# A tuned hybrid-encoder kernel: the final norm of four token tiles done in place between the pieces of a product, residual stores put behind loads, pooled tokens loaded one product sooner

## The chip, the cores and the metric

The kernel runs on one core of a Trainium2 chip. The metric is the time of the core in device microseconds (us) for one execution. TensorE (PE), VectorE (DVE), ScalarE (ACT) and GpSimd (POOL) work side by side, each through its own instructions in order; SyncE (SP) issues nearly all transfers (DMAs), in order too.

## The reference, cut to what matters

One layer with 1024 tokens of 1024 channels, all in float32:

```python
h = rmsnorm(x, norm_mix)
q, k, v, r, lr_f, lr_b, u, g_a, g_b = split(h @ w_in)
y_a = (gla(forward) + gla(backward), normed per head, gated) @ w_branch_gla   # branch A
y_b = (multiscale_pool(u) @ w_pool_group[g], per group g) * pool_scale        # branch B
x = x + (sigmoid(g_a) * y_a + sigmoid(g_b) * y_b) @ w_out
h2 = rmsnorm(x, norm_ffn)
x = x + (silu(h2 @ w_gate) * (h2 @ w_up)) @ w_ffn_out                          # w_ffn_in = [w_gate | w_up]
out = rmsnorm(x, norm_final)       # x * rsqrt(mean(x^2) + eps) * norm_final, per token
```

## The kernel before

Every large product is done by a seven-product scheme on 2 x 2 blocks of both operands, numbered 1 to 7; sums and differences of blocks are formed beside the matmuls. Each of the seven works on operands split in two parts, high and low (`wh`/`wl`, `gh`/`gl`, `oh`/`ol`, `ph`/`pl`): ScalarE casts the high part, VectorE or GpSimd subtracts it from the source to give the low part (`split_to`, L197 and L198), and TensorE takes three matmuls (high x high, low x high, high x low) for one product of tiles (L271, `mm3`). Each matmul is 128x512.

The stages, in the profile's time: norm, projections and attention to about 360 us; the gate units, among which the pooled branch is mixed in (`Gates`, to about 580); the branch product and the merged product with the residual, to about 743; the FFN's gate and up products (`Gated`, to about 1200); and the seven products of the FFN's output, each in six pieces (five of 24 matmuls and one of 12), in the order 1, 2, 6, 5, 3, 7, 4, to about 1384. Then comes the last of the final norm.

The order of instructions on each engine is written by hand: the program's order is the order of each engine. After each `mm3` a counter `pump` goes on by one and releases put-off steps (`soon(delay, step)` puts a step off by so many products) and the next steps of generators that run beside the products (`begin(generator, delay)`; each `yield` gives the number of products until its next step). Tiles come from pools that are given round: 39 slots of 4 KB for each partition (`slot`), five scratch tiles (`t2`), six weight tiles. Whoever writes a tile waits for all who used it before, a store that has not landed among them. On SyncE each DMA also waits until the one eight places before it has landed.

Three places of this program are touched:

- **The gate units** (L1346 on). The run of unit n has seven products; `load_pooled(n - 6)` (L1242) loads the two parts `ph`, `pl` of a group of pooled tokens from `p_out` (L1245), for which `Gates.run` then mixes small products `yb` (ScalarE copies a product's bank to `ga`, L1304; VectorE adds, L1309). Beside the gate units, steps prepare FFN weights: GpSimd forms sums, ScalarE casts `uph` (L630) into a scratch tile, VectorE subtracts `upl` (L621), SyncE stores both to `u_out` (L617). These are a ring through the five `t2` tiles.
- **The residual and the second norm.** `collect_out` adds the merged product to `x2`, squares it on ScalarE (`squares`, L1578) and calls `normed`, which scales `x2` into `xn` (VectorE, for the last tile ScalarE, L1598) and lists a store of `x2` to `x_out`; `flush` issues these stores (L501). `features` (L1520 on) then transposes `xn` on TensorE in groups of four (L1530), ScalarE moves each bank to `hb` (L1533), VectorE forms differences (L1545, L1548), ScalarE casts `gh` (L1511), VectorE or GpSimd subtracts `gl` (L1515). `features(1)` begins 12.7 products late. Unit products copy and add into `g` (L1667, L1669) and apply Silu (L1670).
- **The final norm.** After product 3 tiles 0 to 3 are complete. `whole(t)` (L1810) squares both halves of `x2`, and after a delay forms the scale (`two_scale`: VectorE adds, GpSimd takes the power -0.5) and multiplies by scale and gain into an output slot `res` (L1822, two halves), which is stored whole (L1825). Beside this run product 7's pieces, whose operands are loaded as `wor` and `gor` (L1741, L1742), cast (`oh`) and split, the weight's `ol` by VectorE, the activation's by GpSimd. Tiles 4 to 7 are done in halves after products 7 and 4 (`second_half`, `first_half`).

## Time and profile before

| | |
|---|---|
| median of 3 runs | 1393.41 us (1392.92 to 1393.5) |
| the profiled execution | 1393.17 us, span 1391.4 us |
| granted TensorE clock, mean | 0.998 |
| DMA moved | 243.60 MB, mean 175 GB/s |

A timeline row has the start and duration in us, the engine, the line, the operation, what is written from what, and how many like it were joined (x); in brackets the idle time of the engine ahead of it and what ended that. A windows row has the stretch, its length, each engine's busy time and count (PE, PEld, DVE, ACT, POOL), the granted clock of TensorE, the busy share of the DMA engines and GB/s.

### The profile page before, as it was taken

The numbers are of one execution on the slowest core, as the hardware profiler recorded it, in microseconds if no ns is written. First come the engines' busy times: TensorE is split into PE (matmuls) and PEld (weight loads), VectorE is DVE, ScalarE is ACT, GpSimd is POOL, SyncE is SP. The second block draws the span as 40 slices with busy tenths as digits, with TensorE's granted clock in tenths as the row PEclk, the third lists the DMA queues.
The fourth block names the chain that finished last, engine by engine and source line by source line (L and its number), as shares of the span: only waits on it lengthen the run. The fifth ranks groups of instructions, "written<-read, shape, count | busy, mean of one in ns | idle before, by whom it ended". The sixth has DMA issues, their size and how long they took to land. (4 is left out here: it accounts for less than half of the span.)

```text
span 1391.4 us, 18166 instructions
## 1 busy us (share of the span) xinstructions
PE 1367.6 (98%) x6485; PEld 1143.5 (82%) x6485; DVE 837.3 (60%) x1018; ACT 645.5 (46%) x1176; POOL 750.1 (54%) x556
## 2 busy tenths in 40 slices
PE   8999999999999999999999999999999999999998
PEld 6788999988888888788887788888888888888876
DVE  6364656557736876678783865556556555344464
ACT  6465766655334445554347533333333334443243
POOL 3222717232298546568655276666666667564354
PEclk9999999999999999999999999999999999999999
DMA  6111413312488667996416355555544447965461
GB/s 224 31 53 54 147 60 128 107 47 75 136 242 281 200 209 255 373 403 222 165 57 242 114 174 174 174 175 174 162 151 138 146 142 271 395 246 187 166 238 64
DMA packets 166587, 243.60 MB, mean 175 GB/s; under 512 B 10937, under 2 KB 95969, under 8 KB 166497
## 3 DMA queue, kind: packets, MB, share of 16 engines
q1 hardware_dynamic: 166352, 242.18, 51.3%
q8 instruction: 51, 0.84, 0.2%
q14 instruction: 40, 0.32, 0.1%
q10 hardware_dynamic: 144, 0.26, 0.0%
HBM read 164.55 MB, written 77.86 MB: 174 GB/s over the span
## 5 line engine op out<-in xcount | busy, mean ns | idle before, releaser
L198 POOL TENSOR_TENSOR wl<-fs,wh 128x512 fp32r<-128x512 f32 x120 | 165.8, 1385 | 154.7 <-ACT wh L197 101.8
L271 PE MATMUL ps<-gh,wh 128*128 128x512 f32 x616 | 240.5, 390 | 1.2 <-DVE g L1669 0.6
L271 PE MATMUL ps<-gl,wh 128*128 128x512 f32 x616 | 239.8, 389 | 0.8 <-DVE gl L1515 0.8
L271 PE MATMUL ps<-gh,wl 128*128 128x512 f32 x616 | 239.8, 389 | 0.0
L198 POOL TENSOR_TENSOR wl<-fraw,wh 128x512 fp32r<-128x512 f32 x90 | 129.0, 1433 | 67.5 <-ACT wh L197 59.4
L271 PE MATMUL ps<-hh,wh 128*128 128x512 f32 x376 | 151.7, 403 | 0.0
L271 PE MATMUL ps<-hh,wl 128*128 128x512 f32 x376 | 146.8, 390 | 0.6 <-POOL wl L198 0.6
L271 PE MATMUL ps<-hl,wh 128*128 128x512 f32 x376 | 146.6, 390 | 0.0
L198 POOL TENSOR_TENSOR ol<-gor,oh 128x1024 fp32r<-128x1024 f32 (+1 forms) x42 | 104.5, 2496 | 77.3 <-ACT oh L197 70.3
L271 PEld LDWEIGHTS ps<-gh,wh 128*128 128x128 f32 x616 | 115.7, 188 | 25.9 <-DVE g L1669 0.9
L271 PEld LDWEIGHTS ps<-gl,wh 128*128 128x128 f32 x616 | 115.6, 188 | 24.6 <-DVE gl L1515 1.1
L271 PEld LDWEIGHTS ps<-gh,wl 128*128 128x128 f32 x616 | 115.6, 188 | 24.3 <-DMA wl<-u_out 0.3
L271 PE MATMUL ps<-ol,oh 128*128 128x512 f32 x308 | 120.7, 392 | 2.0 <-DVE ol L198 2.0
L271 PE MATMUL ps<-oh,ol 128*128 128x512 f32 x308 | 120.5, 391 | 0.0
L271 PE MATMUL ps<-oh,oh 128*128 128x512 f32 x308 | 120.4, 391 | 0.0
L198 POOL TENSOR_TENSOR wl<-raw,wh 128x512 fp32r<-128x512 f32 x40 | 54.6, 1377 | 116.2 <-ACT wh L197 107.8
L198 POOL TENSOR_TENSOR wl<-wraw,wh 128x512 fp32r<-128x512 f32 x56 | 89.9, 1632 | 45.6 <-ACT wh L197 45.5
L198 DVE TENSOR_TENSOR ol<-wor,oh 128x1024 fp32r<-128x1024 f32 (+1 forms) x42 | 68.2, 1653 | 47.1 <-ACT oh L197 44.4
L197 ACT CAST wh<-fs 128x512 fp32r<-128x512 f32 x120 | 73.8, 615 | 29.8 <-DVE fs L935 26.3
L271 PEld LDWEIGHTS ps<-hh,wl 128*128 128x128 f32 x376 | 70.6, 188 | 16.2 <-POOL wl L198 1.1
L271 PEld LDWEIGHTS ps<-hh,wh 128*128 128x128 f32 x376 | 70.7, 188 | 13.3 <-ACT wh L197 0.4
L271 PEld LDWEIGHTS ps<-hl,wh 128*128 128x128 f32 x376 | 70.8, 188 | 13.0
(260 smaller groups left out, 3114.5 us busy)
## 6 DMA issues: line engine op xcount, KB each, us to landing
fraw<-in_w_ffn_in_dram SPq DMA_DIRECT2D x44, 512.0 KB, 5.9
gor<-g_out SPq DMA_DIRECT2D x35, 512.0 KB, 5.4
g_out<-s SPq DMA_DIRECT2D x44, 256.0 KB, 2.3
raw<-in_w_in_dram SPq DMA_DIRECT2D x40, 256.0 KB, 4.9
fraw<-in_w_in_dram SPq DMA_DIRECT2D x20, 512.0 KB, 6.6
wor<-t_out SPq DMA_DIRECT2D x20, 512.0 KB
g_out<-g SPq DMA_DIRECT2D x33, 256.0 KB, 2.4
x<-in_x_dram SPq DMA_DIRECT2D x16, 512.0 KB, 4.6
```

The costliest lines, as they stand in the source:

```text
L197: nc.scalar.copy(hi, src)
L198: eng.tensor_tensor(lo, src, as_f32(hi), op=ALU.subtract)
L271: nc.tensor.matmul(ps, a[i], b[j], start=first and n == 0, stop=last and n == 2, skip_group_check=onto)
```

## The change

It makes four edits.

1. `load_pooled` for groups 0 and up is called ahead of the third product of a run, not behind it. On SyncE this moves rows in one place, in the run of unit 8. SyncE there before (`u_out` are stores of prepared weights, `ph` and `pl` the loads of pooled tokens, `yb_out` stores):

```order
L617 DMA u_out_6_517<-uph_5327 128x512
L617 DMA u_out_6_517<-upl_5328 128x512
L617 DMA u_out_3_514<-uph_5358 128x512
L617 DMA u_out_3_514<-upl_5359 128x512
L1245 DMA ph_5401<-p_out 128x1024
L1245 DMA pl_5402<-p_out 128x1024
L501 DMA yb_out<-ga_5128 256x1x512
L501 DMA yb_out<-ga_5151 256x1x512
```

SyncE at the same place now:

```order
L1245 DMA ph_5375<-p_out 128x1024
L1245 DMA pl_5376<-p_out 128x1024
L617 DMA u_out_6_517<-uph_5327 128x512
L617 DMA u_out_6_517<-upl_5328 128x512
L617 DMA u_out_3_514<-uph_5358 128x512
L617 DMA u_out_3_514<-upl_5359 128x512
L501 DMA yb_out<-ga_5128 256x1x512
L501 DMA yb_out<-ga_5151 256x1x512
```

The two loads went ahead of four stores.

2. The stores of the last five tiles of `x2` go behind loads: `normed(late=True)` doesn't flush, and `flush` is put off by three products. SyncE at the end of the merged product before:

```order
L1492 DMA wl_7106<-u_out_2_513 128x512
L501 DMA x_out<-x_1307_6532 128x1024
L501 DMA x_out<-x_1265_6332 128x1024
L501 DMA x_out<-x_1266_6334 128x1024
L501 DMA x_out<-x_1267_6336 128x1024
L501 DMA x_out<-x_1268_6338 128x1024
L1705 DMA wot_7177<-in_w_ffn_out_dram 128x1024
L1705 DMA wol_7178<-in_w_ffn_out_dram 128x1024
L1492 DMA wh_7181<-u_out_2_520 128x512
L1492 DMA wl_7182<-u_out_2_520 128x512
```

and now:

```order
L1494 DMA wl_7106<-u_out_2_513 128x512
L1708 DMA wot_7172<-in_w_ffn_out_dram 128x1024
L1708 DMA wol_7173<-in_w_ffn_out_dram 128x1024
L1494 DMA wh_7176<-u_out_2_520 128x512
L1494 DMA wl_7177<-u_out_2_520 128x512
L501 DMA x_out<-x_1307_6532 128x1024
L501 DMA x_out<-x_1265_6332 128x1024
L501 DMA x_out<-x_1266_6334 128x1024
L501 DMA x_out<-x_1267_6336 128x1024
L501 DMA x_out<-x_1268_6338 128x1024
```

The five stores went behind two loads of the output weight and a pair of split weights.

3. `features(1)` begins 13.2 products late instead of 12.7, and its odd steps take 1.6 products instead of 2. The first transposes stand three matmuls later among TensorE's, the third to the eighth earlier relative to the products. On ScalarE, from the first evacuation (`hb<-tr`) on, before:

```order
L1511 CAST gh_7263<-hb_6983 128x1024
L1533 ACTIVATE hb_7244<-tr_7272,cols 128x512
L1670 ACT_TABLE_LOAD
L1670 ACTIVATE g_7172<-g_7172 128x512
L1533 ACTIVATE hb_7244<-tr_7292,cols 128x512
L1511 CAST gh_7299<-hb_6984 128x1024
L1533 ACTIVATE hb_7245<-tr_7308,cols 128x512
L1670 ACTIVATE g_7174<-g_7174 128x512
L1533 ACTIVATE hb_7245<-tr_7325,cols 128x512
```

and now:

```order
L1513 CAST gh_7266<-hb_6983 128x1024
L1535 ACTIVATE hb_7247<-tr_7272,cols 128x512
L1673 ACT_TABLE_LOAD
L1673 ACTIVATE g_7167<-g_7167 128x512
L1535 ACTIVATE hb_7247<-tr_7292,cols 128x512
L1513 CAST gh_7299<-hb_6984 128x1024
L1535 ACTIVATE hb_7248<-tr_7305,cols 128x512
L1535 ACTIVATE hb_7248<-tr_7315,cols 128x512
L1513 CAST gh_7322<-hb_6983 128x1024
```

The Silu of the second unit's `g` went behind the second evacuation and a cast. VectorE's order changes alike: the first subtraction of L1548 stands ahead of that unit's add into `g` (L1669), and the two adds into `sums` come behind the last two `gl`.

4. The final norm of tiles 0 to 3: the squares write to scratch tiles (in the two other functions too), the scaled rows are written over `x2` instead of into slots `res`, and `whole` is called once, after the fourth tile, and lists twelve steps: for tile n at 1, 6 and 14.5 products plus 9 n the scale, the two multiplications, and the store. VectorE from the end of product 3, before (`ol` are the low halves of weight pieces of product 7 and, last, 4):

```order
L1851 TENSOR_TENSOR x_2138_10763<-ps_11293,x_2138_10763 128x512
L198 TENSOR_TENSOR ol_11725<-wor_11647,oh_11724 128x1024
L1822 SCALAR_TENSOR_TENSOR res_11691<-x_2117_10649,n3rs_11705,gfin_10640 128x512 x2
L1584 TENSOR_SCALAR n3rs_11742<-n3ms_11709 128x1
L1822 SCALAR_TENSOR_TENSOR res_11699<-x_2124_10687,n3rs_11716,gfin_10640 128x512 x2
L1584 TENSOR_SCALAR n3rs_11751<-n3ms_11720 128x1
L1822 SCALAR_TENSOR_TENSOR res_11710<-x_2131_10725,n3rs_11742,gfin_10640 128x512 x2
L1822 SCALAR_TENSOR_TENSOR res_11721<-x_2138_10763,n3rs_11751,gfin_10640 128x512 x2
L198 TENSOR_TENSOR ol_11767<-wor_11683,oh_11766 128x1024
L198 TENSOR_TENSOR ol_11803<-wor_11733,oh_11802 128x1024
L198 TENSOR_TENSOR ol_11839<-wor_11787,oh_11838 128x512
```

and now:

```order
L1860 TENSOR_TENSOR x_2138_10763<-ps_11293,x_2138_10763 128x512
L198 TENSOR_TENSOR ol_11723<-wor_11647,oh_11722 128x1024
L1586 TENSOR_SCALAR n3rs_11737<-n3ms_11702 128x1
L198 TENSOR_TENSOR ol_11750<-wor_11683,oh_11749 128x1024
L1815 SCALAR_TENSOR_TENSOR x_2117_10649<-x_2117_10649,n3rs_11737,gfin_10640 128x512 x2
L1586 TENSOR_SCALAR n3rs_11781<-n3ms_11707 128x1
L198 TENSOR_TENSOR ol_11791<-wor_11731,oh_11790 128x1024
L1815 SCALAR_TENSOR_TENSOR x_2124_10687<-x_2124_10687,n3rs_11781,gfin_10640 128x512 x2
L1586 TENSOR_SCALAR n3rs_11826<-n3ms_11712 128x1
L198 TENSOR_TENSOR ol_11833<-wor_11772,oh_11832 128x512
L1815 SCALAR_TENSOR_TENSOR x_2131_10725<-x_2131_10725,n3rs_11826,gfin_10640 128x512 x2
L1586 TENSOR_SCALAR n3rs_11871<-n3ms_11717 128x1
```

Each pair of multiplications now has an `ol` ahead of it and one behind it. On SyncE the four stores, which stood together ahead of the loads of product 7's last piece and all of product 4's, now stand one by one between those loads: the first behind product 7's last loads, the others behind the first, the third and the fourth pair of loads of product 4.

The diff:

```diff
--- before.py
+++ after.py
@@ -1356,6 +1356,8 @@
         for at, (of, p) in enumerate(run):
             if not gates_ahead.step() and at in (5, 7):
                 line_make()
+            if n >= 6 and at == 2 and not last:
+                load_pooled(n - 6)
             zs[of].run(p)
             for _ in range(2 * (at == 0 and not last)):
                 gunits[n + 1].load()
@@ -1369,7 +1371,7 @@
                 load_pool_weights(n - 5)
             elif n >= 6 and at == 2:
                 split_pool_weights(n - 6)
-            if n >= 6 and at == (0 if last else 2):
+            if n >= 6 and at == 0 and last:
                 load_pooled(n - 6)
             if last and at == 1:
                 load_block(0, 0)
@@ -1551,7 +1553,7 @@
                 low_block(5, k // 2 - 1, block(0, 0, k // 2 - 1), (nc.gpsimd, nc.vector)[k // 2 - 1])
             elif half and k == 6:
                 low_block(6, 0, block(0, 0, 0))
-            yield 2 if half == 0 else 2 if k % 2 else 1.2
+            yield 2 if half == 0 else 1.6 if k % 2 else 1.2
         if half == 0:
             return
 
@@ -1574,9 +1576,9 @@
 
     COLS = slice(0, HALF), slice(HALF, D)
 
-    def squares(t, ms, res, j):
+    def squares(t, ms, j, junk=None):
         nc.scalar.activation(
-            res[:, COLS[j]], x2[t][:, COLS[j]], AF.Square, scale=1.0 / 32.0, accum_out=ms[:, j : j + 1]
+            t2(s="sq")[:, :] if junk is None else junk, x2[t][:, COLS[j]], AF.Square, scale=1.0 / 32.0, accum_out=ms[:, j : j + 1]
         )
 
     def two_scale(ms):
@@ -1589,14 +1591,15 @@
 
     unnormed = []
 
-    def normed(keep=0):
+    def normed(keep=0, late=False):
         while len(unnormed) > keep:
             t = unnormed.pop(0)
             if t != NT - 1:
                 scale_by(xn[t], x2[t][:, :], two_scale(mss[t]))
             else:
                 nc.scalar.activation(xn[t][:, :], x2[t][:, :], AF.Copy, scale=two_scale(mss[t])[:, :])
-            flush()
+            if not late:
+                flush()
             later(x2_out[t], x2[t][:, :])
 
     def collect_out(p, m, ps):
@@ -1609,10 +1612,10 @@
                 mss[t] = vec(2, "n2ms")
                 xn[t] = slot(shape=(D,), s="xn")
             for col in {5: (0, 1), 2: (0,), 3: (1,)}[p]:
-                squares(t, mss[t], xn[t], col)
+                squares(t, mss[t], col, xn[t][:, COLS[col]])
             if p != 2:
                 unnormed.append(t)
-                normed(1)
+                normed(1, p == 3)
 
     def before_out(p):
         if p == 4:
@@ -1636,8 +1639,8 @@
         len(BRANCH) * 2, MERGED, collect_out, before_out, amid_out, (1, 2, 3, 4, 5), (1, 6, 7),
         lambda p: X_BANKS if p == 1 else U_BANKS
     )
-    normed()
-    flush()
+    normed(late=True)
+    soon(3, flush)
 
 
     class Gated:
@@ -1756,7 +1759,7 @@
             both.append((hi, lo))
         ready_pieces.append(both)
 
-    begin(features(1), 12.7)
+    begin(features(1), 13.2)
     zs = {n: Gated(units[n], True) for n in range(3)}
     out_sums, summing = [OutSums(0)], None
 
@@ -1807,50 +1810,56 @@
 
     scales = {}
 
-    def whole(t):
-
-        ms, res = vec(4, "n3ms"), slot(shape=(D,), s="res")
-        for j in range(2):
-            squares(t, ms, res, j)
-
-        def scale():
-            rs = two_scale(ms)
-            soon(1.5, partial(finish, rs))
-
-        def finish(rs):
+    def scaled(t, j):
+        xs = x2[t][:, COLS[j]]
+        nc.vector.scalar_tensor_tensor(
+            xs, xs, scales[t][:, :], gain_final[:, COLS[j]], op0=ALU.mult, op1=ALU.mult
+        )
+
+    def whole(ts):
+
+        mss = {}
+        for t in ts:
+            mss[t] = vec(4, "n3ms")
             for j in range(2):
-                nc.vector.scalar_tensor_tensor(
-                    res[:, COLS[j]], x2[t][:, COLS[j]], rs[:, :], gain_final[:, COLS[j]], op0=ALU.mult, op1=ALU.mult
-                )
-            nc.sync.dma_start(out[t * P : (t + 1) * P, :], res[:, :])
-
-        soon(2, scale)
+                squares(t, mss[t], j)
+
+        def scale(t):
+            scales[t] = two_scale(mss[t])
+
+        def finish(t):
+            for j in range(2):
+                scaled(t, j)
+
+        def store(t):
+            nc.sync.dma_start(out[t * P : (t + 1) * P, :], x2[t][:, :])
+
+        steps = [(at + 9 * n, step, t) for n, t in enumerate(ts) for at, step in ((1, scale), (6, finish), (14.5, store))]
+        for at, step, t in sorted(steps, key=lambda e: e[0]):
+            soon(at, partial(step, t))
 
     def second_half(t):
 
-        ms, res = vec(4, "n3ms"), slot(shape=(D,), s="res")
-        squares(t, ms, res, 1)
+        scales[t] = vec(4, "n3ms")
+        squares(t, scales[t], 1)
         nc.gpsimd.tensor_tensor(x2[t][:, COLS[1]], x2[t][:, COLS[1]], gain_final[:, COLS[1]], op=ALU.mult)
-        scales[t] = ms, res
 
     def first_half(t):
-        ms, res = scales[t]
-        squares(t, ms, res, 0)
-        rs = two_scale(ms)
-        nc.vector.scalar_tensor_tensor(
-            res[:, COLS[0]], x2[t][:, COLS[0]], rs[:, :], gain_final[:, COLS[0]], op0=ALU.mult, op1=ALU.mult
-        )
-        nc.scalar.activation(res[:, COLS[1]], x2[t][:, COLS[1]], AF.Copy, scale=rs[:, :])
+        squares(t, scales[t], 0)
+        scales[t] = two_scale(scales[t])
+        scaled(t, 0)
+        xs = x2[t][:, COLS[1]]
+        nc.scalar.activation(xs, xs, AF.Copy, scale=scales[t][:, :])
         for j, queue in ((0, nc.sync), (1, nc.scalar if t == NT - 1 else nc.sync)):
-            queue.dma_start(out[t * P : (t + 1) * P, COLS[j]], res[:, COLS[j]])
+            queue.dma_start(out[t * P : (t + 1) * P, COLS[j]], x2[t][:, COLS[j]])
 
     def collect(p, m, ps):
 
         half, j = {1: (0, 0), 2: (0, 0), 6: (0, 1), 5: (1, 1), 7: (1, 1), 3: (0, 1), 4: (1, 0)}[p]
         xs = x2[4 * half + m][:, COLS[j]]
         add(xs, ps, xs)
-        if p == 3:
-            whole(m)
+        if p == 3 and m == 3:
+            whole(range(4))
         elif p == 7:
             second_half(4 + m)
         elif p == 4:
```

## The prediction

> **What bounds the kernel now.** I read the busy times first, then the waits of TensorE, then the timeline at each wait, and last the windows with the granted clock.
>
> ```profile
> span 1391.4 us, 18166 instructions
> PE 1367.6 (98%) x6485; PEld 1143.5 (82%) x6485; DVE 837.3 (60%) x1018; ACT 645.5 (46%) x1176; POOL 750.1 (54%) x556
> ```
>
> TensorE is the bound: 1367.6 of 1391.4 us. The change leaves its instructions as they are, so it can only win or lose time in which TensorE waits or runs at a lower clock. The profiled execution took 1393.17 us, 0.24 below the median of the runs (1393.41); the sum below is made against 1393.17. An effect under 0.2%, 2.8 us, can hardly be told from no change here.
>
> The view of TensorE's waits has one long wait in the output products. Its timeline there, and the windows behind it:
>
> ```profile
> 1336.68 0.39 PE L271 MATMUL ps<-oh,ol 128*128 128x512 f32 x1
> 1336.90 0.39 PE L271 MATMUL ps<-oh,oh 128*128 128x512 f32 x1
> 1339.30 0.50 PE L271 MATMUL ps<-ol,oh 128*128 128x512 f32 x1 [2.01 <-DVE ol L198]
> ...
> 1343.53 0.39 PE L271 MATMUL ps<-oh,oh 128*128 128x512 f32 x1
> ```
> ```profile
> 1340.20:1343.50 3.30, 3.30 (x9) 2.61 (x8) 0.88 (x2) 0.97 (x2) 0.00 (x0) 0.50 1.01 335
> ```
>
> Matmuls of this shape start 0.227 us apart at full clock (1336.68 to 1336.90). From 1336.90 to 1343.53 there are 12 starts, worth 2.72 us; they took 6.63. So **3.9 us** are lost: 2.2 in the wait, and about 1.7 because the granted clock (the third column from the end of the windows row) was 0.50 for the 3.3 us after it.
>
> **The final norm.** VectorE's timeline shows what the low half of a weight piece, `ol`, stood behind, and SyncE's shows its queue:
>
> ```profile
> 1324.90 1.23 DVE L198 TENSOR_TENSOR ol<-wor,oh 128x1024 fp32r<-128x1024 f32 x1 [2.64 <-issue]
> 1326.05 3.57 DVE L1822 SCALAR_TENSOR_TENSOR res<-x,n3rs,gfin 128x512 f32<-128x512 f32 x2
> ...
> 1331.11 7.00 DVE L1822 SCALAR_TENSOR_TENSOR res<-x,n3rs,gfin 128x512 f32<-128x512 f32 x4
> 1338.04 2.35 DVE L198 TENSOR_TENSOR ol<-wor,oh 128x1024 fp32r<-128x1024 f32 x2
> ```
> ```profile
> 1325.67 1.04 ACT L197 CAST oh<-wor 128x1024 fp32r<-128x1024 f32 x1
> ```
> ```profile
> 1329.64 8.83 SPq L1825 DMA_DIRECT2D out_dram<-res  x4
> 1338.57 0.38 SPq L1741 DMA_DIRECT2D wor<-t_out  x1
> ```
>
> The `ol` that TensorE needed at 1337.1 had its cast by 1326.7, but it ran at 1338.04, behind eight products with gain and scale, 1.75 us each (7.00 / 4). After the change this `ol` stands ahead of the first pair and is done near 1328. What is late next? A full piece of product 7 has 24 matmuls, 24 x 0.227 = 5.4 us. VectorE has per tile two products, one small scale and one `ol`: 2 x 1.75 + 0.2 + 1.23 = 4.9 us. It keeps ahead of TensorE, and the work enters the loop two pieces ahead. That also is the cover's price: if the in-place products took over 2.0 us each, the spare 0.5 us a piece would be gone. The stores now wait one at a time between loads. The fourth waits for VectorE until about 1347, and behind it stand the loads for the last two pieces of product 4. From 1337.1 TensorE has two and a half pieces of product 7 (13.6 us) and four of product 4 (21.8) ahead of these: over 20 us of cover. Squares into scratch tiles instead of output slots are the same eight instructions. After the last matmul the tail's instructions are the same too; only where they write changes, which I put at nothing (bounds: 0.3 us either way, less than half of one 0.7 us pass). **Term: -3.9 us**; bounds -3.9 and, if half of a wait came back with the low clock, -1.1 (half of 2.2 lost again, and 1.7).
>
> **The middle: late stores of the residual and other times of the transposes.** TensorE between 752 and 776:
>
> ```profile
> 754.11 0.33 PE L1530 MATMUL tr<-ident,xn 128*128 128x128 f32 x1 [0.87 <-ACT xn L1598]
> 757.91 0.50 PE L271 MATMUL ps<-gh,wh 128*128 128x512 f32 x1 [0.51 <-DMA wh<-u_out]
> 765.62 0.66 PE L1530 MATMUL tr<-ident,xn 128*128 128x128 f32 x4
> 766.89 0.50 PE L271 MATMUL ps<-gh,wh 128*128 128x512 f32 x1 [0.62 <-DVE g L1669]
> 775.31 0.50 PE L271 MATMUL ps<-gl,wh 128*128 128x512 f32 x1 [0.76 <-DVE gl L1515]
> ```
> ```profile
> 738.62 12.30 SPq L501 DMA_DIRECT2D x_out<-x  x5
> ...
> 752.35 0.43 SPq L1492 DMA_DIRECT2D wh<-u_out  x1
> ```
>
> The five stores hold the queue from 738.62 to 750.92 while they wait for the last adds; the weight that TensorE wants at 757.4 is asked for only at 752.35. In the new order it is asked for ahead of them, and this wait goes. The first transposes come one group of three matmuls later (0.68 us), which fills most of the 0.87 us. Together some 1.4 us. But this does not reach the end, since ScalarE evacuates the transposes on its own schedule:
>
> ```profile
> 761.97 0.67 ACT L1533 ACTIVATE hb<-tr,cols 128x512 f32<-128x512 f32 x1
> ...
> 764.88 0.68 ACT L1533 ACTIVATE hb<-tr,cols 128x512 f32<-128x512 f32 x1
> 766.87 0.63 ACT L1670 ACTIVATE g<-g 128x512 f32<-128x512 f32 x1 [1.31 <-DVE g L1669]
> ...
> 769.44 1.05 ACT L1511 CAST gh<-hb 128x1024 fp32r<-128x1024 f32 x1 [1.36 <-DVE hb L1548]
> ```
> ```profile
> 766.15 0.68 DVE L1669 TENSOR_TENSOR g<-ps,g 128x512 f32<-128x512 f32 x1
> 768.18 1.23 DVE L1548 TENSOR_TENSOR hb<-hb,hb 128x1024 f32<-128x1024 f32 x1 [1.34 <-ACT hb L1533]
> ...
> 774.03 1.23 DVE L1515 TENSOR_TENSOR gl<-hb,gh 128x1024 fp32r<-128x1024 f32 x1 [0.52 <-ACT gh L1511]
> ```
>
> The eighth transpose needs the bank that the evacuation of 764.88 to 765.56 frees, now as before, when it ran at 765.62. That evacuation ends a chain of casts and subtractions which nothing here starts sooner. TensorE gets there some 1.7 us early (those 1.4, and three matmuls that now stand behind this transpose instead of ahead, 0.8, less a first wait of 0.6 for the evacuation that ends at 762.64). It waits from about 763.9 to 765.6, runs its four transposes (0.36, as from 761.41 to 761.77 in the same view) and three matmuls (0.78 with their start), and begins the next product at about 766.75 instead of 766.89: -0.1. What is won lies behind it. ScalarE no longer puts the Silu of 766.87, which waits for VectorE, between two evacuations; the second one ends at 766.2, and VectorE takes the subtraction `hb` ahead of the add `g`. The add then ends about 768.0 instead of 766.83; the matmuls that need its bank now come one product (12 starts, 2.7 us) after 766.75, so this wait is covered. The low half `gl` that TensorE waited for at 775.31 follows from 766.2 by `hb` 1.23, `gh` 1.05, the Silu and two evacuations (0.63 + 2 x 0.65), `hb` 1.23, `gh` 1.05 and `gl` 1.23: 773.9 instead of 775.25. TensorE reaches it 31 starts after 766.75, at 773.8 to 773.9: the wait goes, and 775.31 becomes about 773.95. **Term: -1.35 us**; bounds -3.1 (if the chain started sooner too, by the 1.7 us) and +0.5 (if the new wait of 1.7 lowers the clock as the 2.01 did, +1.7, and the 0.1 is not had).
>
> **The pooled tokens.** In the run of gate unit 8 the loads of `p_out` go ahead of the four stores `u_out_6` and `u_out_3`. TensorE, SyncE, ScalarE there, and how long stores `u_out` took to land:
>
> ```profile
> 556.18 0.39 PE L271 MATMUL ps<-trh,wl 128*128 128x512 f32 x1
> ...
> 558.04 0.50 PE L271 MATMUL yb<-pl,wph 128*128 128x512 f32 x1 [0.70 <-DMA pl<-p_out]
> 558.38 0.39 PE L271 MATMUL yb<-ph,wpl 128*128 128x512 f32 x1
> ```
> ```profile
> 568.89 0.47 PE L271 MATMUL ps<-trh,wh 128*128 128x512 f32 x1
> ```
> ```profile
> 546.41 0.42 SPq L617 DMA_DIRECT2D u_out<-uph  x1
> ...
> 551.50 0.32 SPq L617 DMA_DIRECT2D u_out<-upl  x1
> ...
> 552.34 0.43 SPq L1245 DMA_DIRECT2D pl<-p_out  x1
> ```
> ```profile
> 551.56 0.62 ACT L630 CAST uph<-fraw 128x512 fp32r<-128x512 f32 x1 [0.65 <-DMA u_out<-upl]
> ...
> 561.96 0.62 ACT L630 CAST uph<-fraw 128x512 fp32r<-128x512 f32 x1 [3.99 <-DMA u_out<-upl]
> ...
> 568.23 0.58 ACT L1304 COPY ga<-ps 128x512 f32<-128x512 f32 x1
> ```
> ```profile
> DMA to landing us min/median/max: 2.6/3.7/7.1
> ```
>
> Three starts (0.68 us) took 2.20 from 556.18 to 558.38: 1.52 us lost. The loads come early enough in the new order to end this: `ph` goes out at 546.4, and `pl` at 551.5, when VectorE frees its slot, with 5 us until it is wanted. But the gain has a wall 10 us on. The matmul of 568.89 starts 0.08 after the copy of 568.23 ends (568.81), and this copy stands on ScalarE behind a ring of casts `uph`, each of which waits for an earlier store `u_out` to land and give its scratch tile back. TensorE comes there 1.5 us early and waits 1.5. And the ring gets later: the four stores go out from 551.9 instead of 546.4 to 551.5, behind `pl`. By the end of the next pair of stores 3.0 MB are then asked for from 551.5 on where it was 2.75; at the 335 GB/s of the windows row of 1340.20, a busy stretch like this one, 0.25 MB more is 0.7 us. **Term: +0.7 us** (-1.5 + 1.5 + 0.7). Bounds: -1.5, if the ring has slack that I don't see; and +4.6: a store issued at 551.9 that lands after the 7.1 us of the slowest one delays the split behind it and its store to about 559.8 instead of 556.9, so 2.9 late, and the wait of over 2.01 us lowers the clock for 1.7.
>
> **Sum:** 1393.17 - 3.9 - 1.35 + 0.7 = 1388.6; with the 0.24 up to the median of the runs it is **1388.8**, the number that the rivals below start from.
>
> **The clock.** The rows on it are the wait of 2.01, after which it was 0.50, and waits of up to 0.87 (754.11), around which the windows show 1.00:
>
> ```profile
> 752.70:754.20 1.50, 0.63 (x6) 0.35 (x4) 0.00 (x0) 1.30 (x2) 0.17 (x1) 1.00 0.97 276
> ```
>
> Of the two new waits the one at 764, some 1.7, lies between these rows, and the one at 567 lies between them at 1.5 and at the upper one only with the whole 0.7 of the ring. The price, 1.7 us each, decides more than any other. I give each drop less than even odds.
>
> The Trainium skill's page "TensorE: Matmul & The Clock Gate" (Part 1, "What's actually happening") gives a free-running window of about 3.4 us and the lower clock after at least one idle window, and in "Why this matters for your kernels" warns only of gaps over about 3 us. By that rule neither new wait would cost a clock and the time would stay 1388.8; but the row of 1340.20 shows 0.50 after 2.01 us, so here the measurement decides against the 3 us.
>
> **Rivals.**
> - *A new wait lowers the clock.* At 567 or 764, one of the two: 1388.8 + 1.7 = 1390.5. For it speaks the row of 2.01; against it the waits up to 0.87. Both: 1392.2.
> - *The pooled loads' gain is kept.* The ring is not later and the copy of 568.23 comes sooner: 1388.8 - 2.2 = 1386.6. Against it stands the slack of 0.08.
> - *The final norm does not do what it says.* The products find VectorE slower in place, or a store holds the loads, and half of the wait returns with its clock: 1388.8 + 2.8 = 1391.6. Against it the 0.5 us a piece and the 20 us.
> - *Slower than before: the ring of scratch tiles.* Between 551.9 and 568.2 it turns three times, and each turn waits for a store to land. If each takes the 7.1 of the slowest row instead of about 5 (the store of 556.9 landed at 561.96), the copy comes 6.3 late, and with the low clock: 1393.41 - 5.25 + 6.3 + 1.7 = 1396.2. It decides once the ring is over 3.5 us late (5.25 without the clock). For it: this queue carries loads of 1 MB ahead of stores in a busy stretch. Against it: the bytes are those of before.
>
> **Chances.** Forecast 0.49; one drop of the clock 0.25, both 0.08; gain kept 0.08; final norm 0.04; the ring 0.06. Faster by over 0.2% means under 1390.6: nearly all of the forecast (0.45), half of the single drop (0.13) and the kept gain (0.08), 0.66. Slower means over 1396.2: half of the ring (0.03) and as much for what I don't see, 0.06. Within 0.2%: 0.28. The range goes from the kept gain, 1386.3, to past both drops, 1393.5, and leaves out the ring and the edges.
>
> **What would show it.** Right: no wait on `ol` near 1337 and no 0.50 there; no wait on `pl<-p_out` at 557, but one of 1.5 to 2.2 on ScalarE's copy near 568; a wait near 764 on the evacuation, none near 775 on `gl`. Wrong: if the copy near 568 starts before 568.2 in the same counting, the term of the pooled tokens has the wrong sign; if windows after 568 or 765 show 0.50, the first rival holds; if a wait on `ol` comes back between 1337 and 1360, VectorE's 4.9 us per piece was too little.

## The result and the profile after

The changed kernel takes **1390.16 us** (median of 10 runs, 1389.23 to 1392.34); the kernel before took 1393.43 beside it (10 runs, 1392.02 to 1394.02). The ratio is 0.9979, interval 0.9969 to 0.9989: 3.3 us faster, where 4.6 had been forecast (1388.8; range 1386.3 to 1393.5). The profiled execution took 1389.48 us, close to the fastest.

The page's first lines and its row of the granted clock, then the view of TensorE's waits (us in total, how often, the longest), both of the changed kernel:

```profile
span 1387.7 us, 18162 instructions
PE 1365.6 (98%) x6485; PEld 1143.0 (82%) x6485; DVE 842.6 (61%) x1018; ACT 644.9 (46%) x1176; POOL 752.6 (54%) x556
PEclk9999999999999999999999999999999999999999
```
```profile
PE vps L428 <- DMA rows<-in_b_decay_bwd_dram: 7.0, 1, 7.0
PE tr L1532 <- ACT hb L1535: 2.1, 2, 1.6
...
PE ps L271 <- ACT ga L1304: 1.1, 2, 0.7
PE ps L271 <- DVE x L1860: 0.9, 1, 0.9
```

The waits on `ol`, `gl` and `pl` that the prediction started from are gone. In their place stand two on ScalarE's evacuation `hb` (the longer 1.6), one more on its copy `ga` (two now, 0.41 and 0.71; one of 0.70 before) and one on VectorE's addition into `x` (0.9). The last of these was not forecast.

To compare executions I add up, for each stage, what TensorE's starts took beyond 0.2267 us for a 128x512 matmul (a quarter of that for a 128x128 transpose). I call this the lost time. It takes in waits, the slower starts right after them, and a lower clock. The sums are taken from rows of the timeline and leave out excesses of a few hundredths. With every start counted the three stages give 2.73, 6.40 and 3.93 before and 1.81, 5.00 and 1.18 after, so the differences hold to about 0.1.

| stage | before | after |
|---|---|---|
| pooled tokens, 556 to 577 us | 2.49 | 1.67 |
| transposes and `gl`, 752 to 777 us | 6.11 | 4.65 |
| output products, 1336 to 1352 us | 3.90 | 1.16 |

That is 5.0 us less, while the span is 3.7 shorter. The other 1.3 lie ahead of these stages, in code that the change does not touch: TensorE's first wait, on a load, is 7.0 instead of 6.6, and the rest is spread over the first 360 us. The profiles of this study differ there by up to 1.9, whichever edits they have. The 0.8 of the first row is not the worth of the earlier loads either: of six profiles that have them and five scratch tiles, two lost 1.7 there and four 2.6 to 3.0. What divides the six stands under pool_only.

**The output products.** VectorE from the end of product 3, GpSimd beside it, and TensorE where it waits:

```profile
1325.74 2.73 DVE L198 TENSOR_TENSOR ol<-wor,oh 128x1024 fp32r<-128x1024 f32 x1 [0.49 <-ACT oh L197]
1328.91 3.56 DVE L1815 SCALAR_TENSOR_TENSOR x<-x,n3rs,gfin 128x512 f32<-128x512 f32 x2 [0.44 <-POOL n3rs L1587]
...
1334.16 3.54 DVE L1815 SCALAR_TENSOR_TENSOR x<-x,n3rs,gfin 128x512 f32<-128x512 f32 x2 [0.44 <-POOL n3rs L1587]
...
1338.86 2.44 DVE L1815 SCALAR_TENSOR_TENSOR x<-x,n3rs,gfin 128x512 f32<-128x512 f32 x2 [0.45 <-POOL n3rs L1587]
...
1343.00 5.69 DVE L1815 SCALAR_TENSOR_TENSOR x<-x,n3rs,gfin 128x512 f32<-128x512 f32 x2 [0.44 <-POOL n3rs L1587]
1348.61 1.21 DVE L198 TENSOR_TENSOR ol<-wor,oh 128x1024 fp32r<-128x1024 f32 x1
1349.75 2.47 DVE L1860 TENSOR_TENSOR x<-ps,x 128x512 f32<-128x512 f32 x4
```
```profile
1328.85 2.40 POOL L198 TENSOR_TENSOR ol<-gor,oh 128x1024 fp32r<-128x1024 f32 x1
...
1334.10 2.39 POOL L198 TENSOR_TENSOR ol<-gor,oh 128x1024 fp32r<-128x1024 f32 x1
...
1338.80 1.29 POOL L198 TENSOR_TENSOR ol<-gor,oh 128x512 fp32r<-128x512 f32 x1
1341.51 1.46 POOL L1587 TENSOR_TENSOR n3rs<-n3rs,half_neg 128x1 f32<-128x1 f32 x1 [1.41 <-DVE n3rs L1586]
1342.94 5.20 POOL L198 TENSOR_TENSOR ol<-gor,oh 128x1024 fp32r<-128x1024 f32 x2
```
```profile
1349.27 0.39 PE L271 MATMUL ps<-oh,ol 128*128 128x512 f32 x1
1350.57 0.47 PE L271 MATMUL ps<-oh,oh 128*128 128x512 f32 x1 [0.92 <-DVE x L1860]
```

The same pair of multiplications takes 3.56, 3.54, 2.44 and 5.69 us. Each begins 0.06 us after a GpSimd subtraction begins, and outlasts it: the subtractions take 2.40, 2.39, 1.29, and 5.20 for two back to back. Take these off and 1.16, 1.15, 1.15 and 0.49 are left. The fourth pair meets two subtractions because GpSimd took the power (`n3rs`, 1341.51) ahead of them, which waited for VectorE's step before it. VectorE then comes to the additions at 1349.75, and TensorE waits for the output bank that the first of them frees.

In the kernel before, VectorE had this row between the two that the prediction shows:

```profile
1329.66 1.40 DVE L1822 SCALAR_TENSOR_TENSOR res<-x,n3rs,gfin 128x512 f32<-128x512 f32 x2
```

A pair without a subtraction beside it took 1.40 there too, 0.70 each. The 7.00 for four joined two of about 0.73 and two of about 2.88.

**The middle and the pooled tokens.** TensorE at the last two groups of transposes, and after the pooled products:

```profile
763.09 0.66 PE L1532 MATMUL tr<-ident,xn 128*128 128x128 f32 x4 [0.51 <-ACT hb L1535]
766.01 0.66 PE L1532 MATMUL tr<-ident,xn 128*128 128x128 f32 x4 [1.57 <-ACT hb L1535]
```
```profile
568.46 0.40 PE L271 MATMUL yb<-ph,wpl 128*128 128x512 f32 x1
569.27 0.50 PE L271 MATMUL ps<-trh,wh 128*128 128x512 f32 x1 [0.41 <-ACT ga L1304]
```

The weights `wh` are now asked for at 743.82, ahead of the stores, and the wait on them is gone; the eighth group of transposes waits instead, as forecast. The clock over it (first row; third column from the end), and behind the old place of the wait on `ol` (second row), is 1.00:

```profile
766.70:768.70 2.00, 2.00 (x10) 1.61 (x10) 1.77 (x2) 0.80 (x1) 0.00 (x0) 1.00 0.19 61
...
1336.90:1343.50 6.60, 6.60 (x31) 5.47 (x30) 5.71 (x9) 3.16 (x3) 4.19 (x4) 1.00 0.92 330
```

### The profile page after: what moved, and what is told of

It is laid out like the page before. It is cut to its first block, busy times and chain, and to the rows that moved or that the text cites. A ratio compares the mean times of both kernels' runs of the same rounds, so it can differ in the third digit from the quotient of the medians.

```text
span 1387.7 us, 18162 instructions
## 1 busy us (share of the span) xinstructions
PE 1365.6 (98%) x6485; PEld 1143.0 (82%) x6485; DVE 842.6 (61%) x1018; ACT 644.9 (46%) x1176; POOL 752.6 (54%) x556
```

## Experiments

Lost time by stage in the profile of each kernel (us), and its time:

| kernel | 556–577 | 752–777 | 1336–1354 | median, us (runs) |
|---|---|---|---|---|
| before | 2.49 | 6.11 | 3.90 | 1393.43 (10) |
| after | 1.67 | 4.65 | 1.16 | 1390.16 (10) |
| pool_only | 2.85 | 6.24 | 3.88 | 1394.16 (11) |
| mid_only | 2.11 | 4.63 | 3.87 | 1392.35 (11) |
| final_only | 2.75 | 6.23 | 1.21 | 1391.52 (11) |
| features_only | 2.28 | 4.67 | 2.28 | 1392.09 (1) |
| stores_only | 1.16 | 6.24 | 2.27 | 1391.19 (1) |
| scales_first | 2.95 | 6.29 | 0 | 1389.25 (8) |
| no_gp_two | 1.74 | 4.70 | 0 | 1387.64 (1) |
| split_gap | 2.58 | 4.77 | 0 | 1388.06 (5) |
| split_gap_old_loads | 2.65 | 4.71 | 0 | 1388.25 (6) |
| small_four | 2.84 | 6.13 | 1.21 | 1391.56 (1) |
| ring_six | 1.01 | 4.56 | 1.17 | 1388.36 (1) |
| ring_six_split | 0.58 | 4.87 | 0 | 1386.40 (5) |

Where the time ahead of a stage moved it by a microsecond or so, the window follows the stage. pool_only to final_only and scales_first were timed beside 30 runs of the kernel before (median 1393.15), the two of split_gap beside 10 (1392.92), ring_six_split beside 9 (1392.72); their ratios are to these.

### One edit at a time

**pool_only**: edit 1 alone.

```diff
+            if n >= 6 and at == 2 and not last:
+                load_pooled(n - 6)
...
-            if n >= 6 and at == (0 if last else 2):
+            if n >= 6 and at == 0 and last:
```

> Only the loads of pooled tokens go sooner; the rest is the kernel before. Theory of the prediction (the ring of scratch tiles gets later by the four stores behind the loads): the wait on pl<-p_out near 557 is gone, a wait of 1.5 to 2.2 us on ScalarE's copy stands near 568, and the time is 0 to 0.7 us above the kernel before. Rival (the ring has slack, so that part of the gain is kept, as the changed kernel's profile hints with a wait of only 0.41 us there): the wait near 568 stays under 1 us and the time is 0.8 to 1.5 us below.

Ratio 1.0004, interval 0.9995 to 1.0013: no gain, and a loss of 0 to 0.7 can't be told from none. TensorE no longer waits at 557, but behind the pooled products:

```profile
570.53 0.50 PE L271 MATMUL ps<-trh,wh 128*128 128x512 f32 x1 [1.57 <-ACT ga L1304]
```

The same wait is 1.57, 1.70, 1.60 and 1.30 here, in scales_first, small_four and split_gap, but 0.41 and 0.49 in the changed kernel and no_gp_two. The traces show what divides them. The load of `pl` goes out 0.02 to 0.03 us after VectorE's subtraction `upl` ends, in all six, and the four stores `u_out` stand behind that load. VectorE and GpSimd in the changed kernel, then in small_four:

```profile
550.88 0.69 DVE L621 TENSOR_TENSOR upl<-fraw,uph 128x512 fp32r<-128x512 f32 x1 [4.94 <-ACT wh L197]
```
```profile
550.94 1.79 POOL L198 TENSOR_TENSOR wl<-fraw,wh 128x512 fp32r<-128x512 f32 x1 [0.36 <-ACT wh L197]
```
```profile
550.66 1.77 DVE L621 TENSOR_TENSOR upl<-fraw,uph 128x512 fp32r<-128x512 f32 x1 [5.08 <-ACT wh L197]
```
```profile
550.58 1.30 POOL L198 TENSOR_TENSOR wl<-fraw,wh 128x512 fp32r<-128x512 f32 x1 [0.36 <-DMA u_out<-upl]
```

Where VectorE begins 0.01 to 0.06 us ahead of GpSimd, `upl` takes 0.69, the loads of `ph` and `pl` stand 4.0 to 4.1 us apart, and ScalarE's cast `uph` waits 5.0 for the store. Where GpSimd begins up to 0.3 ahead, `upl` takes 1.55 to 1.81, the loads stand 5.2 apart, and the cast waits 5.8 to 6.1. So the order of two starts within a fraction of a microsecond decides about 1 us of the wait at the copy.

**mid_only**: edits 2 and 3.

```diff
-            yield 2 if half == 0 else 2 if k % 2 else 1.2
+            yield 2 if half == 0 else 1.6 if k % 2 else 1.2
...
-    begin(features(1), 12.7)
+    begin(features(1), 13.2)
...
-    normed()
-    flush()
+    normed(late=True)
+    soon(3, flush)
```

> Only the late stores of the residual and the new times of the second features. Theory (what is won early is handed back on the eighth transpose, and the wait on gl near 775 goes): 1.3 to 1.5 us below the kernel before, with a wait of about 1.6 us near 765 and the clock at 1.00 behind it. Rival (that wait lowers the clock): a windows row of 0.50 behind 765 and a time within 0.5 us of the kernel before.

Ratio 0.9995 (0.9987 to 1.0004). The lost time of the stage falls by 1.48, with the clock at 1.00; the median falls by 0.8. The interval holds the expected 1.3 to 1.5 and no change at all, so the gain is shown by the profile and not by the times.

**final_only**: edit 4 alone.

```diff
+        steps = [(at + 9 * n, step, t) for n, t in enumerate(ts) for at, step in ((1, scale), (6, finish), (14.5, store))]
```

> Only the new final norm. Theory from the changed kernel's profile (the wait near 1337 and its low clock go, 3.9 us, and a wait of about 0.9 us comes back at the start of product 4, since VectorE's fourth pair of multiplications is held up by two subtractions on GpSimd): 2.5 to 3 us below the kernel before, the fourth pair at 5 to 6 us against 3.5 of the first two. Rival (the new wait belongs to the other edits): 3.9 us below, no wait near 1350.

Ratio 0.9987 (0.9978 to 0.9996). The lost time falls by 2.7, and the new wait on the addition stands here too (0.97 us), so it comes from this edit alone. The expected 5 to 6 us of the fourth pair did not come. VectorE, and GpSimd's second subtraction:

```profile
1345.68 3.55 DVE L1812 SCALAR_TENSOR_TENSOR x<-x,n3rs,gfin 128x512 f32<-128x512 f32 x2 [0.44 <-POOL n3rs L1585]
1349.15 3.41 DVE L198 TENSOR_TENSOR ol<-wor,oh 128x1024 fp32r<-128x1024 f32 x1
```
```profile
1348.86 2.62 POOL L198 TENSOR_TENSOR ol<-gor,oh 128x1024 fp32r<-128x1024 f32 x1 [0.84 <-ACT oh L197]
```

Here the second subtraction meets the next `ol` instead, which takes 3.41 for 1.21. Pair and `ol` together take as long as in the changed kernel (6.96 and 6.90), and VectorE comes to the additions just as late. So it is not the slow pair as such that makes TensorE wait, but two subtractions between the late power and the additions, whichever of VectorE's instructions they hold up.

**features_only** and **stores_only** divide mid_only: the first takes the two numbers of its diff, the second the late stores.

> The kernel before with only the two numbers of the features' transposes and the late product changed, the stores where they were. Theory (these numbers alone take the wait on gl away): no wait on gl near 775 us, loss between 752 and 777 us lower by 1.3 to 1.5 us than in the kernel before (6.1 us). Rival (the gain in the middle comes from the late stores): the wait of 1.4 us on gl stays.

> The kernel before with only the five stores of the residual put behind the loads. Theory (the weights come sooner, but the transposes wait for ScalarE's evacuation all the same): no wait on the weights near 757 us, a loss of 4.6 to 4.9 us between 752 and 768 us as in the kernel before (4.72), and the wait of 1.4 us on gl near 775 us stays; time within 0.5 us of the kernel before. Rival (the late stores carry the gain of the middle): the loss between 752 and 777 us is lower by 1 us or more.

The numbers alone bring the whole gain (6.11 to 4.67); the late stores bring nothing (6.24). In stores_only the weights come in time, and the eighth group of transposes waits 0.92 instead; in features_only TensorE waits 1.14 for the weights and 0.74 for the evacuation. The single times (1391.19 and 1392.09) cannot be read against the medians, for a reason that their profiles show; the expected time of stores_only, within 0.5 of the kernel before, was missed by 1.0 for it. TensorE and the windows of stores_only at the old wait on `ol`:

```profile
1338.81 0.50 PE L271 MATMUL ps<-ol,oh 128*128 128x512 f32 x1 [2.00 <-DVE ol L198]
1339.14 0.39 PE L271 MATMUL ps<-oh,ol 128*128 128x512 f32 x1
```
```profile
1339.00:1341.00 2.00, 2.00 (x10) 1.61 (x10) 0.89 (x1) 0.00 (x0) 0.00 (x0) 1.00 0.97 295
```

The same wait of 2.0 us, and the clock stays at 1.00; in features_only too. Of the five profiles with this wait, three show the low clock (before, pool_only, mid_only; 3.9 lost) and two do not (2.3).

### Why the multiplications are slow

**scales_first**: the changed kernel with all four scales formed at once, so that no power stands between GpSimd's subtractions.

```diff
-        steps = [(at + 9 * n, step, t) ...
+        steps = [(at + 9 * n * (step is not scale), step, t) ...
```

> The changed kernel with all four scales formed at once after the squares, so that no multiplication and no GpSimd subtraction waits for a power on GpSimd; pairs and stores stay where they are. Theory (the late powers put two GpSimd subtractions side by side under the fourth pair): the fourth pair takes 3.5 us or less, the wait at the start of product 4 is gone, and the time is about 1.2 us below the changed kernel, near 1389. Rival (the pair is slow for another reason, such as writing in place): the fourth pair still takes over 5 us and the time is that of the changed kernel, near 1390.2.

The wait on the addition is gone; the ratio to before is 0.9971 (0.9961 to 0.9981). The pairs take 1.41, 5.70, 3.54 and 1.41 us: the slow one is now the second, where a delay of VectorE costs nothing. But this profile has the low clock in the middle, after a wait of the length that had left it at 1.00 in the changed kernel:

```profile
766.80 1.03 PE L1532 MATMUL tr<-ident,xn 128*128 128x128 f32 x4 [1.58 <-ACT hb L1535]
...
768.06 0.63 PE L271 MATMUL ps<-gl,wh 128*128 128x512 f32 x1
768.48 0.63 PE L271 MATMUL ps<-gh,wl 128*128 128x512 f32 x1
```
```profile
767.00:769.40 2.40, 2.40 (x9) 2.02 (x9) 2.24 (x3) 1.04 (x2) 0.00 (x0) 0.50 0.03 7
```

**no_gp_two**: GpSimd is kept away from the fourth pair and from the `ol` behind it. This kernel leaves out the low part of two pieces of the activation: ScalarE writes the whole value into both places.

```diff
-            split_to(hi[:, :c, :], lo[:, :c, :], src[:, :c, :], eng)
+            if n in (36, 37) and eng is nc.gpsimd:
+                nc.scalar.copy(hi[:, :c, :], src[:, :c, :])
+                nc.scalar.copy(lo[:, :c, :], src[:, :c, :])
+            else:
+                split_to(hi[:, :c, :], lo[:, :c, :], src[:, :c, :], eng)
```

> The changed kernel with GpSimd's subtraction of the first two pieces of the fourth product replaced by copies on ScalarE; this leaves out the low part of these pieces, the whole value stands in its place. Theory (VectorE's pair of scalings stands still while GpSimd subtracts): the pair of the fourth tile takes 1.4 to 2.0 us instead of 5.69, and TensorE's wait of 0.92 us on the addition near 1350 us goes. Rival (the pair is slow for another reason, such as ScalarE's or the stores' traffic): the pair still takes over 5 us and the wait stays.

VectorE of no_gp_two; the first three pairs still stand beside subtractions, the fourth does not:

```profile
1328.17 3.55 DVE L1819 SCALAR_TENSOR_TENSOR x<-x,n3rs,gfin 128x512 f32<-128x512 f32 x2 [0.45 <-POOL n3rs L1587]
...
1338.13 2.44 DVE L1819 SCALAR_TENSOR_TENSOR x<-x,n3rs,gfin 128x512 f32<-128x512 f32 x2 [0.44 <-POOL n3rs L1587]
...
1342.27 1.41 DVE L1819 SCALAR_TENSOR_TENSOR x<-x,n3rs,gfin 128x512 f32<-128x512 f32 x2 [0.44 <-POOL n3rs L1587]
```

1.41 instead of 5.69, the three others as before, and no wait on the addition. The next `ol` takes 1.22, and VectorE now idles 2.09 us ahead of the additions. So GpSimd's subtractions are what makes VectorE slow and TensorE wait.

### The long wait near 766, and the ring

**split_gap**: scales_first with one number more, so that the last transposes come one product earlier and the long wait falls apart.

```diff
-            yield 2 if half == 0 else 1.6 if k % 2 else 1.2
+            yield 2 if half == 0 else 1.6 if k % 2 else 2.2 if k == 6 else 1.2
```

> The changed kernel with all four scales at once (as in scales_first) and the last transposes of the features' second half due after six products instead of seven, so that the wait of 1.57 us near 765 us is cut into shorter ones. Theory (that one long wait lowers the clock in some executions and makes the spread of 1389.2 to 1392.3 us): no wait over 1.1 us near 765 us, granted clock 1.00 there, about 0.8 us of the wait on gl near 773 us comes back; median 1388 to 1389 us and the runs within 1.5 us of each other. Rival (the spread comes from elsewhere, such as the front or the loads): median as scales_first (1389.25 us) or later, and the same spread of some 3 us.

Ratio 0.9968 (0.9955 to 0.998). The waits near 766 are 0.53 and 0.88, on `gl` 0.33 comes back, the clock is 1.00, and five runs lie within 1.7 us. The median is 1.2 below that of scales_first, timed in another batch; the expected 0.8 on `gl` came to 0.3, and the spread is just over the expected 1.5. That a clock without drops is the reason for the narrower spread is likely, not shown: in final_only the mean clock was 0.999 in all 11 runs, and they still lay 2.6 us apart.

**split_gap_old_loads**: split_gap without edit 1.

> split_gap without the earlier loads of the pooled tokens. Theory (that the gain at the pooled loads is handed back at the ScalarE copy near 568 us): the wait on pl near 557 us is back with 1.5 us, the wait near 568 us is gone, and the time is that of split_gap within 0.7 us. Rival (the earlier loads are worth their 1.5 us): 1.3 to 1.6 us slower than split_gap.

1388.25 against 1388.06, ratio to before 0.9969 (0.9957 to 0.9981): by the medians the earlier loads are worth 0.2, which five and six runs can't tell from nothing.

**ring_six**, its control **small_four** (second line of the diff only), and **ring_six_split** (both lines on top of split_gap):

```diff
-    tmp = ctx.enter_context(tc.tile_pool(name="tmp", bufs=5))
-    small = ctx.enter_context(tc.tile_pool(name="small", bufs=5))
+    tmp = ctx.enter_context(tc.tile_pool(name="tmp", bufs=6))
+    small = ctx.enter_context(tc.tile_pool(name="small", bufs=4))
```

> The changed kernel with six scratch tiles t2 instead of five; to make room, four tiles instead of five in the ring of small tiles that also holds the pool weights. Theory (the gain at the pooled loads is handed back because ScalarE's copy stands behind casts that wait for a scratch tile, and so for a store that has not landed): with a sixth tile ScalarE's wait of some 5 us near 552 us gets shorter and the copy near 568 us comes earlier, so TensorE's loss near 568 us (0.69 us in the changed kernel's profile, 1.6 to 2.0 us in three others) falls under 0.4 us. Rival (the copy is late for another reason, such as VectorE's or GpSimd's part of the preparation): ScalarE's wait and TensorE's loss stay as they are.

> The control of ring_six: the changed kernel with five scratch tiles and four small tiles. Theory: the smaller ring of small tiles does nothing, so the waits near 552 and 568 us are those of the changed kernel, and the time lies within 1389 to 1392.5 us. Rival: the smaller ring moves these waits by itself, and ring_six has to be read against this run.

> split_gap with six scratch tiles and four small tiles, as in ring_six. Theory of the ring: the gain of the earlier pooled loads, 1.3 to 1.5 us, is now kept, so 1386.5 to 1387.2 us, against 1388.06 for split_gap. Rival (the gain is handed back elsewhere, by the next wait on ScalarE's copies near 575 us or by the front): 1388 us or more.

ScalarE of small_four, then of ring_six, at the same casts and the same copy:

```profile
557.97 0.62 ACT L630 CAST uph<-fraw 128x512 fp32r<-128x512 f32 x1 [6.09 <-DMA u_out<-upl]
...
569.46 0.58 ACT L1304 COPY ga<-ps 128x512 f32<-128x512 f32 x1
```
```profile
555.85 0.62 ACT L630 CAST uph<-fraw 128x512 fp32r<-128x512 f32 x1 [4.62 <-DMA u_out<-uph]
...
567.67 0.58 ACT L1304 COPY ga<-ps 128x512 f32<-128x512 f32 x1
```

With a sixth scratch tile the copy comes 1.8 us sooner than in small_four, 1.0 sooner than in the changed kernel (568.64), and TensorE's lost time behind the pooled products (1.88 in small_four, 0.69 in the changed kernel) is gone. ring_six_split takes 1386.40 us, ratio 0.9956 (0.9942 to 0.997), 1.7 below split_gap. The two were timed in different batches and their intervals overlap, but its slowest run (1386.88) is faster than the fastest of split_gap (1387.43). This fits the theory of the ring, by which the gain of the earlier loads then stays. It is the fastest kernel of the study, and beats both kernels compared. What a sixth tile brings without the earlier loads was not tried, so how the 1.7 divides between the two stays open.

## Why the prediction was right or wrong

- **The final norm: mechanism right, size wrong** (-3.9 forecast, -2.74 in the profile). The wait on `ol` and its low clock went, as said. The step that failed is "2 x 1.75 + 0.2 + 1.23 = 4.9 us. It keeps ahead of TensorE". The 1.75 was a mean over multiplications that had GpSimd beside them (2.88 each) and ones that had not (0.73). A pair alone takes 1.41, beside one subtraction 3.55, beside two 5.69; and the sum left out the 0.44 that VectorE idles for each power. The fourth tile, from its scale's step at 1341.23 to the next `ol` at 1348.61, takes 7.4 us where 5.4 were at hand. The price was a wait of 0.92 at 1350, 1.16 lost. The text had named this sign ("a wait on `ol` comes back between 1337 and 1360"), though the wait was for the addition. The rival, that half the wait and its clock return, came true by 1.16 of its 2.8.
- **The lock.** A pair takes 1.41 alone, and beside a subtraction the whole length of that plus 1.15, so hardly anything of the pair runs meanwhile. The Trainium skill's page "SBUF — State Buffer" ("SBUF: two separate sides") says that a VectorE instruction with two inputs in SBUF and a GpSimd instruction that reads SBUF exclude each other for the whole instruction. The runs agree.
- **The starting point.** The 3.9 is what one execution lost. In two of five profiles the same wait cost 2.3, because the clock held. The 49 runs of the kernel before in the three batches point the same way in the mean: the 17 with a mean clock of 0.999 average 1392.41 us, the 32 at 0.997 or 0.998 average 1393.38. So the median could not fall by the whole 3.9. final_only fell by 1.6, between 2.3 - 1.2 = 1.1 and 3.9 - 1.2 = 2.7.
- **The middle: right** (-1.35; measured -1.46, and -1.48 alone). The wait on `wh` goes and is handed back at the eighth group of transposes: 752 to 767 lost 4.98 before and 4.79 after with every start counted, where -0.1 was said, and the wait is 1.57 where 1.7 was. The wait on `gl` goes. What the text did not separate is that the numbers of edit 3 bring all of it.
- **The pooled tokens: mechanism right, size not told from nothing** (+0.7; about +0.2 in the mean). The gain of 1.5 comes back at the copy, behind the ring. The forecast sign, a wait of 1.5 to 2.2 there, was 0.41 in the changed kernel's own profile and 1.57 to 1.70 in three others. Six profiles with the early loads and five scratch tiles lost 1.67, 2.85, 2.95, 1.74, 2.58 and 2.84 in this stage (mean 2.44), six without them 2.49, 2.11, 2.75, 2.28, 2.65 and 1.16 (mean 2.24). The means differ by less than the profiles of either group do. The 0.7 was worked out from bytes at the rate of the queue; what moved the copy by about 1 us from one profile to the next was the order of VectorE's and GpSimd's starts, which the text did not have.
- **The clock after the new waits: two of six, as the chances had it.** The wait near 766 lowered it in two of six profiles (scales_first, small_four), at 6.29 and 6.13 against 4.6 to 4.7, so 1.5 to 1.6 us; 1.7 was forecast. A rule by the length of the gap alone, as the 3 us of the Trainium skill's page "TensorE: Matmul & The Clock Gate" ("Why this matters for your kernels"), does not fit these runs: 1.57 to 1.58 us gave both, and 2.0 us too. What does fit them stands in the last section.
- **Not forecast:** 1.3 us in the first part of the profiled execution.

Worked out again with what was measured, the sum is 1393.17 - 2.74 - 1.46 + 0.2 = 1389.2, and 1390.8 with the low clock near 766. The ten runs lie from 1389.2 to 1392.3. Of the 1.4 between 1388.8 and their median the terms give 0.6 (1.2 missing in the final norm, less 0.5 and 0.1 that the other two were better); the clock and the first part are left for the rest, and how it divides is not shown. That the profiled execution came within 0.9 of the sum's 1388.6 is partly luck: 1.2 missing in the final norm and 1.3 more in the first part stood against 1.5 that the pooled tokens were better than forecast in this one execution.

## What to carry to other kernels

Take the duration of an instruction from rows whose neighbours on the other engines are those that it will have after the move: a mean over joined rows (7.00 for four) hid a factor of four between single ones (0.73 and 2.88). When a wait is taken away, look for the next shared resource with a fixed schedule, a ring of buffers or an evacuation, since the gain is kept only where that has room; here the kernel with one more scratch tile was 1.7 us faster, where the earlier loads alone had brought nothing. And a loss that depends on the clock should be priced over several executions, not one: in some of them the same wait doesn't cost it.

## What the runs showed of the hardware

- The clock's drop is not decided by the length of the wait alone. After 2.0 us idle it fell to 0.50 in three of five profiles, after 1.57 to 1.58 near 766 in two of six, after 1.57 to 1.70 near 568 in none of three (pool_only, small_four, scales_first). The traces show what decides. In each of them the changes of the granted clock stand a whole number of steps of 3.413 us apart (before: 1340.06, 1343.47 and 1387.85, one step and thirteen), and each low stretch inside the kernel lasts one step. Cut at these steps, the stretches with the least work for TensorE are, in before, small_four, stores_only, the changed kernel and features_only (two in a row; PE's busy time is the third number):

```profile
1336.65:1340.06 3.41, 1.40 (x6) 0.85 (x5) 3.41 (x3) 0.00 (x0) 0.92 (x1) 1.00 0.36 132
```
```profile
763.16:766.57 3.41, 1.58 (x8) 0.88 (x7) 1.58 (x2) 2.12 (x4) 0.06 (x1) 1.00 0.24 90
```
```profile
1335.20:1338.61 3.41, 1.61 (x8) 0.99 (x6) 3.41 (x2) 0.00 (x0) 1.86 (x1) 1.00 0.04 18
```
```profile
764.03:767.44 3.41, 1.84 (x11) 1.25 (x10) 2.29 (x3) 2.21 (x3) 0.00 (x0) 1.00 0.02 5
```
```profile
1335.09:1338.51 3.42, 2.44 (x11) 1.69 (x9) 3.42 (x3) 0.00 (x0) 2.71 (x1) 1.00 0.01 2
1338.51:1341.92 3.41, 2.38 (x10) 1.99 (x11) 2.11 (x2) 0.00 (x0) 0.00 (x0) 1.00 0.80 255
```

  The first two were followed by 0.50, the others were not. Behind the first 20 us and ahead of TensorE's last work, all five steps with 1.40 to 1.58 busy were followed by 0.50 (1.40 in before, pool_only and mid_only, 1.48 in scales_first, 1.58 in small_four), and no step with 1.61 or more was, in any of the fourteen traces. In features_only the wait of 2.01 fell across two steps, so neither was idle enough. One step fits less well: in ring_six_split the one at the end of TensorE's work (1375.72 to 1379.13) had 1.50 and was not followed by 0.50. Since a wait falls anywhere among the steps, the same wait costs the clock in some executions and not in others.
- A VectorE multiplication of two operands in SBUF and a GpSimd subtraction do not share time: 1.41 us for two of 128x512 alone, 3.55 beside a subtraction of 2.4. VectorE's `ol` of 128x1024 takes 1.21 alone and 2.73 where a subtraction was already running (1325.74). Which of the two began first decided who was held up: 0.06 us ahead, VectorE's `upl` took 0.69 and GpSimd's subtraction 1.79; 0.08 behind, 1.77 and 1.30.
- GpSimd's power on a tile of 128x1 took 0.93 to 1.53 us in the changed kernel's output products, against 2.4 for a subtraction of 128x1024.
